# Two channel MLPs of a diffusion backbone on one core: block products by Strassen's seven instead of eight

## The chip, the cores and the metric

The kernel runs on one core of a Trainium2 chip. The metric is the time of one execution on the device in microseconds (us), lower is better. A core has five engines that each run their own queue in order: TensorE (PE, with its weight loads PEld), VectorE (DVE), ScalarE (ACT), GpSimd (POOL) and SyncE (SP), which issues the DMAs. They wait for each other by semaphores.

## The reference, cut to what matters

Two layers work on 1024 tokens of 1024 channels. Each ends in a channel MLP with 4096 hidden channels; layer 0 has retention and attention before it, layer 1 spatial gating.

```python
def sq_relu_mlp(h, w1, w2):
    return jnp.square(jax.nn.relu(h @ w1)) @ w2
...
        x = x + g1 * o_lat
        x = x + g2 * sq_relu_mlp(modulate(rms_norm(x, norm2_g[l]), sh2, sc2), ff_w1[l], ff_w2[l])
```

The six vectors `sh1 .. g2` of a layer come from a product of the conditioning vector with `mod_w`. Everything is float32.

## The kernel before

Tokens lie along the free axis (two halves `hf` of H = 512), channels on the 128 partitions in KT = 8 chunks. A float32 product is made of three matmuls of rounded parts: a value is split into `hi` (an ACT cast) and `lo` (a DVE subtraction), and `mm3` (L53 to L55) multiplies hi*hi, hi*lo and lo*hi into PSUM. PSUM has two buffers of two banks, tag `mm`, and four of one bank, tag `aux`.

The stages follow each other: start, retention projections (`r_group`), attention projections (`a_group`), attention, `out_proj` 0 (tile `po`), MLP 0 (`up`, `dn`, and `dl` for the last group), the gating's products `pv` and `pu`, `out_proj` 1, MLP 1. In an MLP, `up_both` makes one hidden chunk c of 128 channels for both halves: 2 x 24 matmuls into one buffer, then Relu on ACT (L689), a square on DVE (L690) and a split into `s`. `down` takes two chunks at a time into each of the eight output chunks m, 12 matmuls into a buffer of two banks, and DVE adds the buffer, times g2, to the residual `xt[m]` in SBUF (L725). Up of the next chunks and down of the former ones alternate; the last four chunks go half by half (`dl`, L747), with `done` storing each chunk.

`norm_fin` makes the normalised halves as a generator (`later`, `tick`) that is written between the products: sum of squares on ACT and POOL (L166, L167), `nsum` on PE, a power on POOL (L177), a broadcast `nbc` on PE, then two DVE operations and one of ACT per chunk. The first four up tiles of an MLP need the first half only. The modulation vectors other than the first two are 10 parts of 9 steps (`mod_steps`: a 512 KB load and a DVE accumulation of 128x1024 at L117, then transposes), taken one at a time in the projections (`mod_run(1)`) and two at a time in MLP 0 (`mod_run(2)`).

The order on each engine is not the order of the code: the framework's scheduler places instructions, and tiles of a tag are taken in turn from its buffers.

## Time and profile before

| | us |
|---|---|
| three runs | 2440.36, 2443.74, 2444.03 |
| median | 2443.74 |
| span of the profiled execution, first to last instruction | 2437.2 |
| its PE busy | 2387.2 |
| its DVE / ACT / POOL busy | 1280.7 / 683.0 / 178.5 |

The profiled execution is a run of its own. The span is what its page is made from; its time on the device beside the span is not given, and the median of the three runs is 6.5 us over the span. Busy time of PE counts pipelined matmuls whose rows overlap.

### The profile page before, as it was taken

How to read it: one execution, taken by the hardware profiler on the slowest of the kernel's cores; microseconds unless marked ns; L12 is line 12 of the kernel's file. 1: busy time of each engine (PE TensorE's matmuls, PEld its weight loads, DVE VectorE, ACT ScalarE, POOL GpSimd, SP SyncE). 2: the span in 40 equal slices, each digit the busy share in tenths (PEclk: the TensorE clock that was granted, in tenths of full speed). 3: DMA queues.
4: the chain of work that ended last, by engine and by line, in shares of the span. 5: the costliest groups of instructions: out<-in, count | busy, mean ns of one | idle time of the engine just before them, and what ended most of it. 6: DMA issues, size and time to landing. Idle time of an engine off the chain costs nothing.

```text
span 2437.2 us, 27145 instructions
## 1 busy us (share of the span) xinstructions
PE 2387.2 (98%) x11180; PEld 1941.2 (80%) x11180; DVE 1280.7 (53%) x1776; ACT 683.0 (28%) x1131; POOL 178.5 (7%) x143
## 2 busy tenths in 40 slices
...
GB/s 292 121 37 102 106 83 139 120 44 35 147 95 53 72 92 121 51 105 121 26 138 44 65 100 57 48 122 93 59 39 52 52 35 61 44 47 49 44 26 70
DMA packets 67597, 195.38 MB, mean 80 GB/s; under 512 B 7440, under 2 KB 15120, under 8 KB 67472
## 3 DMA queue, kind: packets, MB, share of 16 engines
...
q8 instruction: 88, 1.44, 0.2%
...
## 4 chain that ended last, share of the span: by engine, by line
PE 88%; DVE 5%; DMA 3%; ACT 2%; POOL 1%; issue 1%; SPq 0%; DVEq 0%; POOLq 0%; ACTq 0%
PE up L53 9%; PE up L55 9%; PE up L54 9%; PE dn L55 8%; PE dn L53 8%; PE dn L54 8%; PE po L53 2%; PE po L54 2%; PE po L55 2%; PE pl L55 2%; PE pl L53 2%; PE pl L54 2%; DMA mw<-in_mod_w 2%; PE pv L55 1%; PE dl L53 1%; PE pv L54 1%
## 5 line engine op out<-in xcount | busy, mean ns | idle before, releaser
L58 ACT CAST wh_w<-st_w 128x1024 fp32r<-128x1024 f32 x128 | 132.7, 1050 | 848.9 <-PE dn L54 396.6
L53 PE MATMUL dn<-s,wh_w 128*128 128x512 f32 x896 | 353.8, 395 | 1.6 <-DVE xa L725 1.6
L55 PE MATMUL dn<-s,wl_w 128*128 128x512 f32 x896 | 353.6, 395 | 0.2 <-DVE wl_w L59 0.2
L54 PE MATMUL dn<-s,wh_w 128*128 128x512 f32 x896 | 353.4, 394 | 0.0
L59 DVE TENSOR_TENSOR wl_w<-st_w,wh_w 128x1024 fp32r<-128x1024 f32 x128 | 159.5, 1261 | 316.7 <-ACT wh_w L58 316.1
L725 DVE SCALAR_TENSOR_TENSOR xb<-dn,mcol,xb 128x1024 f32<-128x1024 f32 x112 | 143.6, 1282 | 127.2 <-PE dn L55 127.1
L53 PE MATMUL up<-hm,wh_w 128*128 128x512 f32 x512 | 202.7, 396 | 0.0
L53 PE MATMUL up<-hn,wh_w 128*128 128x512 f32 x512 | 202.5, 395 | 0.0
L55 PE MATMUL up<-hn,wl_w 128*128 128x512 f32 x512 | 202.4, 395 | 0.0
L54 PE MATMUL up<-hn,wh_w 128*128 128x512 f32 x512 | 202.3, 395 | 0.0
L55 PE MATMUL up<-hm,wl_w 128*128 128x512 f32 x512 | 202.3, 395 | 0.0
L54 PE MATMUL up<-hm,wh_w 128*128 128x512 f32 x512 | 202.2, 395 | 0.0
L53 PEld LDWEIGHTS dn<-s,wh_w 128*128 128x128 f32 x896 | 168.7, 188 | 41.4 <-DVE xa L725 2.1
L55 PEld LDWEIGHTS dn<-s,wl_w 128*128 128x128 f32 x896 | 168.7, 188 | 40.2 <-DVE wl_w L59 0.8
L54 PEld LDWEIGHTS dn<-s,wh_w 128*128 128x128 f32 x896 | 168.8, 188 | 39.3
L725 DVE SCALAR_TENSOR_TENSOR xa<-dn,mcol,xa 128x1024 f32<-128x1024 f32 x112 | 143.5, 1282 | 92.5 <-PE dn L55 92.3
L53 PE MATMUL pl<-wh_g,h 128*128 128x512 f32 x384 | 154.0, 401 | 0.0
L55 PE MATMUL pl<-wh_g,h 128*128 128x512 f32 x384 | 151.9, 396 | 0.0
L54 PE MATMUL pl<-wl_g,h 128*128 128x512 f32 x384 | 151.3, 394 | 0.0
L167 POOL TENSOR_TENSOR ss<-ss,sq 128x512 f32<-128x512 f32 x42 | 62.4, 1487 | 1097.1 <-ACT sq L166 1097.1
L689 ACT ACTIVATE r<-up 128x512 f32<-128x512 f32 x128 | 69.9, 591 | 178.4 <-PE up L55 178.3
L690 DVE TENSOR_TENSOR r<-r 128x512 f32<-128x512 f32 x128 | 83.0, 684 | 68.8 <-ACT r L689 68.8
...
## 6 DMA issues: line engine op xcount, KB each, us to landing
st_w<-in_w SPq DMA_DIRECT2D x128, 512.0 KB, 3.6
mw<-in_mod_w SPq DMA_DIRECT2D x96, 512.0 KB, 4.0
st_wo<-in_wo SPq DMA_DIRECT2D x32, 512.0 KB, 3.5
st_g<-in_wg SPq DMA_DIRECT2D x24, 512.0 KB, 4.7
x<-in_xT SPq DMA_DIRECT2D x8, 512.0 KB, 9.6
xa<-in_xT SPq DMA_DIRECT2D x8, 512.0 KB, 7.4
st_wv<-in_wv SPq DMA_DIRECT2D x8, 512.0 KB, 4.2
xp_d<-xa SPq DMA_DIRECT2D x16, 256.0 KB, 2.0
```

The source lines that it names most:

```text
L53: nc.tensor.matmul(ps, lhsT=a_hi, rhs=b_hi, start=first, stop=False)
L54: nc.tensor.matmul(ps, lhsT=a_hi, rhs=b_lo, start=False, stop=False)
L55: nc.tensor.matmul(ps, lhsT=a_lo, rhs=b_hi, start=False, stop=last)
L58: nc.scalar.copy(hi, src)
L59: eng.tensor_tensor(lo, src, hi.bitcast(F32), ALU.subtract)
L167: eng.tensor_tensor(ss, ss, sq, ALU.add)
L689: nc.scalar.activation(r, ps[:, f * H:(f + 1) * H], AF.Relu)
L690: nc.vector.tensor_tensor(r, r, r, ALU.mult)
L725: nc.vector.scalar_tensor_tensor(xt[m], ps.rearrange("p a b -> p (a b)"), mods[(l, 5)][:, m:m + 1], xt[m], ALU.mult, ALU.add)
```

## The change

Both operands of an MLP product are cut into 2x2 blocks and multiplied by Strassen's method in Winograd's form: seven block products for eight, with sums of blocks formed before and after. For the up product, w1 is cut by input chunks (even and odd k) and by pairs of hidden chunks, p = 0 to 15; the tokens are cut into halves. The weight sums `S1 .. S4` are formed on DVE for each p (`w_forms`), the token sums `T1 .. T4` once per MLP (`norm_forms`, which replaces `norm_fin`; `T3` and `T4` on POOL). `block` is one block product: 12 matmuls of 512 columns for four tiles of 128 channels.

Up and down are two phases now. `up_first` makes two of the seven products of p = 0 to 3 from the first half of the tokens and keeps them in DRAM. `mlp_up` makes for each p seven block products in one `mm` buffer (banks a and b) and one `aux` buffer e, adds them up on DVE, takes Relu and Square on ACT, forms the down product's `B` and `T` and stores all seven in DRAM (`s_d`). `mlp_down` loads them again into the 28 buffers of `fpool`, splits them, and works in jobs (q, p0, p1): output chunks q and q + 4, hidden pairs p0 to p1 - 1, at most four. The residual goes to DRAM in `out_proj` (`x1_d`) and comes back as `xd` at the start of the down phase. The norm at the end of layer 0 comes after the whole MLP. The modulation steps all run in the projections. The diff, cut, without its empty lines and the removed functions:

```diff
                 if gi:
-                    mod_run(1)
+                    mod_run(2 + t)
...
+    mod_run(1000)
...
+    FORMS = ("B11", "T2", "B21", "T3", "T1", "T4", "B22")
+    fpool, close_f = open_pool("fpool", side="right", reuse_waits="tile")
+    def f_tile(name, dtype=F32R):
+        return fpool.tile([P, 2, H], dtype, tag="f", bufs=28, name=name)
+    def block(ps, W, F, first):
+        n = len(F)
+        for t in range(n):
+            c = slice(t * P, (t + 1) * P)
+            mm3(ps, W[:, 0, c], W[:, 1, c], F[t][:, 0, :], F[t][:, 1, :], first and t == 0, t == n - 1, not first)
...
+    def w_forms(src, name, skip=False, eng=nc.vector):
+        R1 = w_raw(src(0), f"ra_{name}")
+        R2 = w_raw(src(1), f"rb_{name}")
+        w = R1.shape[-1]
+        f = {}
+        if not skip:
+            f["A11"] = w_form(R1[:, 0], f"w0_{name}")
+        s1 = tmp(f"s1_{name}")[:, :w]
+        eng.tensor_tensor(s1, R2[:, 0], R2[:, 1], ALU.add)
+        s2 = tmp(f"s2_{name}")[:, :w]
+        eng.tensor_tensor(s2, s1, R1[:, 0], ALU.subtract)
+        f["S2"] = w_form(s2, f"w1_{name}")
+        if not skip:
+            f["A12"] = w_form(R1[:, 1], f"w2_{name}")
+        eng.tensor_tensor(R2[:, 0], R1[:, 0], R2[:, 0], ALU.subtract)
+        f["S3"] = w_form(R2[:, 0], f"w3_{name}")
+        f["S1"] = w_form(s1, f"w4_{name}")
+        f["A22"] = w_form(R2[:, 1], f"w5_{name}")
+        eng.tensor_tensor(R1[:, 1], R1[:, 1], s2, ALU.subtract)
+        f["S4"] = w_form(R1[:, 1], f"w6_{name}")
+        return f
...
+                nc.sync.dma_start(x1_d[m, :, sl], xt[m][:, sl])
+                norm_acc(nt, ss[hf], xt[m][:, sl], m == 0)
...
+            later(norm_forms(l, hf, ss[hf], xt, F))
...
+    def norm_forms(l, hf, ss, xt, F):
+        sl = slice(hf * H, (hf + 1) * H)
+        rs = norm_rstd(nt, ss, H)
+        yield 1
+        pb = norm_bc(rs, H)
+        gs, sh = mods[(l, 4)], mods[(l, 3)]
+        for t in range(4):
+            for j in range(2):
+                k = 2 * t + j
+                x = xt[k][:, sl]
+                nc.vector.scalar_tensor_tensor(x, x, gs[:, k:k + 1], pb, ALU.mult, ALU.mult)
+                nc.scalar.activation(x, x, AF.Identity, bias=sh[:, k:k + 1])
+            def form(n, src, eng=nc.vector):
+                o = f_tile(f"{n}_{l}_{t}")
+                F.setdefault(n, []).append(o)
+                split(src, o[:, 0, :], o[:, 1, :], eng)
+            if hf == 0:
+                form("B11", xt[2 * t][:, sl])
+                form("B21", xt[2 * t + 1][:, sl])
+            else:
+                b11, b21 = xt[2 * t][:, 0:H], xt[2 * t + 1][:, 0:H]
+                b12, b22 = xt[2 * t][:, H:], xt[2 * t + 1][:, H:]
+                t1, t2 = tmp(f"t1_{l}{t}"), tmp(f"t2_{l}{t}")
+                nc.vector.tensor_tensor(t1, b12, b11, ALU.subtract)
+                nc.vector.tensor_tensor(t2, b22, t1, ALU.subtract)
+                form("T2", t2)
+                nc.gpsimd.tensor_tensor(b12, b22, b12, ALU.subtract)
+                form("T3", b12, nc.gpsimd)
+                form("T1", t1)
+                nc.gpsimd.tensor_tensor(b21, b21, t2, ALU.subtract)
+                form("T4", b21, nc.gpsimd)
+                form("B22", b22)
+            yield 1
+    def mlp_up(l, F, s_d, utemp, pro):
+        def src(p):
+            return lambda i: I["w1"][l, p, i]
+        for p in range(16):
+            f = w_forms(src(p), f"u{l}_{p}", skip=p in pro)
+            ps = mm_tile([P, 2, H], f"up{l}_{p}")
+            a, b = ps[:, 0, :], ps[:, 1, :]
+            e = aux_tile([P, H], f"ue{l}_{p}")
+            def act(t):
+                nc.scalar.activation(t, t, AF.Relu)
+                nc.scalar.activation(t, t, AF.Square)
+            def put(n, t):
+                nc.sync.dma_start(s_d[p][FORMS.index(n)], t)
+            e1, s11 = utemp(f"e1_{l}_{p}"), utemp(f"s11_{l}_{p}")
+            if p in pro:
+                nc.sync.dma_start(e1, pro[p])
+                nc.sync.dma_start(s11, s_d[p][0])
+            else:
+                block(a, f["A11"], F["B11"], True)
+                nc.scalar.copy(e1, a)
+            block(b, f["S2"], F["T2"], True)
+            u2 = utemp(f"u2_{l}_{p}")
+            nc.vector.tensor_tensor(u2, b, e1, ALU.add)
+            if p not in pro:
+                block(a, f["A12"], F["B21"], False)
+                nc.scalar.activation(s11, a, AF.Relu)
+                nc.scalar.activation(s11, s11, AF.Square)
+                put("B11", s11)
+            block(b, f["S3"], F["T3"], False)
+            u3 = utemp(f"u3_{l}_{p}")
+            nc.vector.tensor_tensor(u3, b, e1, ALU.add)
+            block(e, f["S1"], F["T1"], True)
+            nc.vector.tensor_tensor(u3, e, u3, ALU.add)
+            act(u3)
+            put("B22", u3)
+            block(b, f["A22"], F["T4"], False)
+            nc.vector.tensor_tensor(e1, b, e1, ALU.add)
+            act(e1)
+            block(e, f["S4"], F["B22"], False)
+            nc.vector.tensor_tensor(u2, e, u2, ALU.add)
+            act(u2)
+            t1, t2 = utemp(f"q1_{l}_{p}"), utemp(f"q2_{l}_{p}")
+            nc.vector.tensor_tensor(t1, u2, s11, ALU.subtract)
+            put("T1", t1)
+            nc.vector.tensor_tensor(t2, u3, t1, ALU.subtract)
+            put("T2", t2)
+            nc.vector.tensor_tensor(u2, u3, u2, ALU.subtract)
+            put("T3", u2)
+            t4 = utemp(f"q4_{l}_{p}")
+            nc.vector.tensor_tensor(t4, e1, t2, ALU.subtract)
+            put("B21", e1)
+            put("T4", t4)
+    def up_first(l, F, s_d, e_d):
+        for p0 in (0, 2):
+            ps = mm_tile([P, 2, H], f"uf{l}_{p0}")
+            W = []
+            for d in range(2):
+                R = w_raw(I["w1"][l, p0 + d, 0], f"rf{l}_{p0 + d}")
+                W.append([w_form(R[:, j], f"wf{l}_{p0 + d}_{j}") for j in range(2)])
+            for d in range(2):
+                block(ps[:, d, :], W[d][0], F["B11"], True)
+                e1 = tmp(f"ef{l}_{p0 + d}")
+                nc.scalar.copy(e1, ps[:, d, :])
+                nc.sync.dma_start(e_d[p0 + d], e1)
+            for d in range(2):
+                block(ps[:, d, :], W[d][1], F["B21"], False)
...
+    def mlp_down(l, xt, s_d, done):
         S = {}
+        def load_s(p):
+            S[p] = {}
+            for i, n in enumerate(FORMS):
+                o = f_tile(f"s{n}_{l}_{p}")
+                lo = o[:, 1, :]
+                nc.sync.dma_start(lo.bitcast(F32), s_d[p][i])
+                split(lo.bitcast(F32), o[:, 0, :], lo)
+                S[p][n] = o
+        def job(q, p0, p1):
+            for p in range(p0, p1):
+                if p not in S:
+                    load_s(p)
+            F = {n: [S[p][n] for p in range(p0, p1)] for n in FORMS}
...
+            f = w_forms(lambda i: I["w2"][l, q, i, :, :, p0:p1], name)
...
+            x11, x12 = xt[q][:, :H], xt[q][:, H:]
+            x21, x22 = xt[q + 4][:, :H], xt[q + 4][:, H:]
+            ps = mm_tile([P, 2, H], f"dn{name}")
+            a, b = ps[:, 0, :], ps[:, 1, :]
+            e = aux_tile([P, H], f"de{name}")
...
+            block(a, f["A11"], F["B11"], True)
+            e1, e2 = tmp(f"e1{name}"), tmp(f"e2{name}")
+            nc.scalar.activation(e1, a, AF.Copy, scale=g1)
+            nc.scalar.activation(e2, a, AF.Copy, scale=g2)
+            add(x21, e2)
+            block(b, f["S2"], F["T2"], True)
+            stt(e1, b, g1, e1)
+            add(x12, e1)
+            block(a, f["A12"], F["B21"], False)
+            stt(x11, a, g1, x11)
+            block(b, f["S3"], F["T3"], False)
+            stt(e2, b, g2, e2)
+            add(x22, e2)
+            block(e, f["S1"], F["T1"], True)
+            stt(x22, e, g2, x22)
+            block(b, f["A22"], F["T4"], False)
+            stt(x21, b, g2, x21)
+            block(e, f["S4"], F["B22"], False)
+            stt(x12, e, g1, x12)
...
+        job(1, 0, 1)
+        job(2, 0, 2)
+        job(3, 0, 3)
+        for i in range(16):
+            job(i % 4, i, min(i + 4, 16))
+    def layer_mlp(l, F, close_xt, s_d, e_d, x1_d, done):
+        up_first(l, F, s_d, e_d)
+        drain()
+        close_xt()
+        up, close_up = open_pool("up", reuse_waits="tile")
+        mlp_up(l, F, s_d, lambda n: up.tile([P, H], F32, tag="u", bufs=16, name=n), {p: e_d[p] for p in range(4)})
+        close_up()
+        xd, close_xd = open_pool("xd", reuse_waits="tile")
+        xt = [xd.tile([P, T], F32, name=f"xd{l}_{m}") for m in range(KT)]
+        for m in range(KT):
+            nc.sync.dma_start(xt[m], x1_d[m])
+        mlp_down(l, xt, s_d, lambda q: done(q, xt))
+        return close_xd, xt
...
+    close_xd, xt = layer_mlp(0, F, close_xa, s_d, e_d, x1_d, done0)
+    hm = [[None] * KT for _ in range(2)]
+    for hf in range(2):
+        rs = norm_rstd(nt, ss1[hf], H)
+        pb = norm_bc(rs, H)
```

**Place 1, the start of MLP 0.** POOL's queue before, where the norm of the second half ends; `ss001` is its sum of squares, `rs` the power, `ss010` the sum at the end of MLP 0.

```order
L167 TENSOR_TENSOR ss001_5523<-ss001_5523,sq_6096 128x512 [waits Activation_49,Pool_49]
L167 TENSOR_TENSOR ss001_5523<-ss001_5523,sq_6131 128x512 [waits Activation_49,Pool_49]
L177 TENSOR_TENSOR rs_6200<-ms_6198,mhalf_76 128x4 [waits DVE_49]
L167 TENSOR_TENSOR ss010_6138<-ss010_6138,sq_10363 128x512 [waits PE_49,Activation_49]
L167 TENSOR_TENSOR ss010_6138<-ss010_6138,sq_10381 128x512 [waits Activation_49,Pool_49]
```

POOL's queue now; `xa` are the residual's chunks, which hold the normalised tokens at this point (second half: b12, b22).

```order
L168 TENSOR_TENSOR ss001_5752<-ss001_5752,sq_6384 128x512 [waits Activation_49,Pool_49]
L178 TENSOR_TENSOR rs_6552<-ms_6550,mhalf_76 128x4 [waits DVE_49]
L746 TENSOR_TENSOR xa0_5722<-xa1_5723,xa0_5722 128x512 [waits DMAHW1_49,DMAHW0_49,DMAHW6_49,DVE_49,Activation_49]
L749 TENSOR_TENSOR xa1_5723<-xa1_5723,t2_00_6564 128x512 [waits DMAHW3_49,DVE_49]
L746 TENSOR_TENSOR xa2_5724<-xa3_5725,xa2_5724 128x512 [waits DMAHW2_49,DMAHW4_49,DVE_49,Activation_49]
L59 TENSOR_TENSOR T3_0_0_6571<-xa0_5722,T3_0_0_6571 128x512 [waits DMAHW7_49,Activation_49]
...
L746 TENSOR_TENSOR xa6_5728<-xa7_5729,xa6_5728 128x512 [waits DMAHW2_49,DMAHW1_49,DVE_49]
L59 TENSOR_TENSOR T4_0_2_6628<-xa5_5727,T4_0_2_6628 128x512 [waits PE_49,Activation_49]
L749 TENSOR_TENSOR xa7_5729<-xa7_5729,t2_03_6639 128x512 [waits DVE_49]
L59 TENSOR_TENSOR T3_0_3_6646<-xa6_5728,T3_0_3_6646 128x512 [waits PE_49,Activation_49]
L59 TENSOR_TENSOR T4_0_3_6653<-xa7_5729,T4_0_3_6653 128x512 [waits PE_49,Activation_49]
```

Sixteen operations of 128x512 now stand behind the power (rows of t = 1 and 2 in between are left out). ACT's queue at the same place, before: `hm0_1` are the chunks of the second half, `r` and `s0` belong to up tiles.

```order
L195 ACTIVATE hm0_1_4_5518<-hp_6297,mcol03_2069 128x512 [waits DVE_49]
L195 ACTIVATE hm0_1_5_5519<-hp_6301,mcol03_2069 128x512 [waits DVE_49]
L689 ACTIVATE r_6344<-up0_3_0_6319 128x512 [waits DVE_49,PE_49,Pool_49]
L195 ACTIVATE hm0_1_6_5520<-hp_6305,mcol03_2069 128x512 [waits DVE_49]
L195 ACTIVATE hm0_1_7_5521<-hp_6309,mcol03_2069 128x512 [waits DVE_49]
L58 CAST s0_3_0_6347<-r_6344 128x512 [waits DVE_49]
```

And now; `w1_u0_0` is W S2 of p = 0, which `up0_0`, the first tile of `mlp_up`, needs.

```order
L58 CAST T2_0_3_6642<-t2_03_6639 128x512 [waits DVE_49]
L58 CAST T3_0_3_6646<-xa6_5728 128x512 [waits Pool_49]
L58 CAST T1_0_3_6649<-t1_03_6638 128x512
L58 CAST T4_0_3_6653<-xa7_5729 128x512 [waits Pool_49]
L58 CAST B22_0_3_6656<-xa7_5729 128x512
L58 CAST w1_u0_0_6671<-s2_u0_0_6669 128x512 [waits DVE_49]
```

The cast of the first weight form stands behind casts that wait for POOL.

**Place 2, the middle of the up phase, PE.** Before: `up0_8` is one hidden chunk, its halves go into its two banks, `up0_9` takes the other buffer.

```order
L55 MATMUL dn0_4_7_7136<-s0_5_1_6735,wl_w2_0_5_7035 128x512
L53 MATMUL up0_8_7156<-hm0_0_0_5506,wh_w1_0_8_7152 128x512 [waits DVE_49]
...
L55 MATMUL up0_8_7156<-hm0_0_7_5513,wl_w1_0_8_7153 128x512
L53 MATMUL up0_8_7156<-hm0_1_0_5514,wh_w1_0_8_7152 128x512
...
L55 MATMUL up0_8_7156<-hm0_1_7_5521,wl_w1_0_8_7153 128x512
L53 MATMUL up0_9_7229<-hm0_0_0_5506,wh_w1_0_9_7225 128x512 [waits DVE_49,Activation_49]
```

Now: `up0_6` is the buffer of p = 6 with banks a and b, `ue0_6` and `ue0_8` are e of p = 6 and 8, `w1` to `w6` the weight forms S2, A12, S3, S1, A22, S4.

```order
L55 MATMUL up0_6_7460<-T2_0_3_6642,w1_u0_6_7440 128x512
L53 MATMUL up0_6_7460<-B21_0_0_6138,w2_u0_6_7443 128x512 [waits DVE_49]
...
L55 MATMUL up0_6_7460<-B21_0_3_6276,w2_u0_6_7443 128x512
L53 MATMUL up0_6_7460<-T3_0_0_6571,w3_u0_6_7447 128x512 [waits Activation_49]
...
L55 MATMUL up0_6_7460<-T3_0_3_6646,w3_u0_6_7447 128x512
L53 MATMUL ue0_8_7759<-T1_0_0_6574,w4_u0_8_7748 128x512 [waits Activation_49]
L53 MATMUL up0_6_7460<-T4_0_0_6578,w5_u0_6_7453 128x512 [waits DVE_49]
...
L55 MATMUL up0_6_7460<-T4_0_3_6653,w5_u0_6_7453 128x512
L53 MATMUL ue0_6_7461<-B22_0_0_6581,w6_u0_6_7457 128x512 [waits DVE_49]
```

Four blocks on one buffer stand behind each other, each with a wait for DVE or ACT at its first matmul; before, a tile's two halves ran through and the wait of the next tile was for the other buffer.

**Place 3, the change from up to down, PE.** Before, the first down tiles: `dn0_0_0` and `dn0_0_1` are output chunks 0 and 1 of the first two hidden chunks.

```order
L55 MATMUL up0_3_1_6443<-hm0_1_7_5521,wl_w1_0_3_6316 128x512
L53 MATMUL dn0_0_0_6486<-s0_0_0_6190,wh_w2_0_0_6476 128x512 [waits DMAHW1_49,DMAHW7_49,DMAHW0_49,Activation_49]
...
L55 MATMUL dn0_0_0_6486<-s0_1_1_6409,wl_w2_0_1_6483 128x512
L53 MATMUL dn0_0_1_6500<-s0_0_0_6190,wh_w2_0_0_6476 128x512 [waits Activation_49]
...
L55 MATMUL dn0_0_1_6500<-s0_1_1_6409,wl_w2_0_1_6483 128x512
L53 MATMUL dn0_0_2_6514<-s0_0_0_6190,wh_w2_0_0_6476 128x512 [waits DVE_49]
```

Now: `ue0_15` ends the up phase, `dnd0_2_0` is the buffer of job (2, 0, 2), `dnd0_1_0` that of job (1, 0, 1), `ded0_3_0` the e of job (3, 0, 3).

```order
L55 MATMUL ue0_15_8802<-B22_0_3_6656,w6_u0_15_8798 128x512
L53 MATMUL dnd0_2_0_9093<-sB11_0_0_8939,w0_d0_2_0_9066 128x512 [waits DVE_49]
...
L55 MATMUL dnd0_2_0_9093<-sB11_0_1_9034,w0_d0_2_0_9066 128x512
L53 MATMUL dnd0_2_0_9093<-sT2_0_0_8943,w1_d0_2_0_9073 128x512 [waits Activation_49]
...
L55 MATMUL dnd0_2_0_9093<-sT2_0_1_9038,w1_d0_2_0_9073 128x512
L53 MATMUL dnd0_2_0_9093<-sB21_0_0_8947,w2_d0_2_0_9076 128x512 [waits DVE_49]
...
L55 MATMUL dnd0_2_0_9093<-sB21_0_1_9042,w2_d0_2_0_9076 128x512
L53 MATMUL ded0_3_0_9210<-sT1_0_0_8955,w4_d0_3_0_9199 128x512 [waits Activation_49]
...
L55 MATMUL ded0_3_0_9210<-sT1_0_2_9166,w4_d0_3_0_9199 128x512
L53 MATMUL dnd0_1_0_8998<-sT3_0_0_8951,w3_d0_1_0_8985 128x512 [waits DVE_49]
```

Blocks of six matmuls on one buffer follow each other, each with a wait at its head, where tiles of twelve with two buffers in turn stood before.

## Rows read from the trace of the kernel before

**Rows 1.** The page: busy us, share of the span, instructions, per engine.
```profile
PE 2387.2 (98%) x11180; PEld 1941.2 (80%) x11180; DVE 1280.7 (53%) x1776; ACT 683.0 (28%) x1131; POOL 178.5 (7%) x143
```
**Rows 2.** Windows of MLP 0, MLP 1 and its end: columns in the first row.
```profile
core 0: us, PE busy (x) PEld busy (x) DVE busy (x) ACT busy (x) POOL busy (x), PEclk, DMA share, GB/s
702.00:1382.00 680.00, 678.19 (x2945) 547.80 (x2945) 358.63 (x378) 138.59 (x193) 2.80 (x2) 1.00 0.25 81
...
1716.00:2388.00 672.00, 672.00 (x2897) 543.41 (x2896) 299.26 (x313) 135.70 (x192) 3.02 (x2) 1.00 0.14 44
2388.00:2437.00 49.00, 45.43 (x195) 36.10 (x193) 14.61 (x20) 2.31 (x4) 0.00 (x0) 1.00 0.23 86
```
**Rows 3.** Timeline of PE in MLP 1: start, duration; first and last of 25.
```profile
1799.75 0.39 PE L53 MATMUL up<-hn,wh_w 128*128 128x512 f32 x1
...
1805.35 0.39 PE L53 MATMUL up<-hn,wh_w 128*128 128x512 f32 x1
```
**Rows 4.** The page's costliest groups: busy us, mean ns, idle before and its releaser.
```profile
L53 PE MATMUL dn<-s,wh_w 128*128 128x512 f32 x896 | 353.8, 395 | 1.6 <-DVE xa L725 1.6
...
L53 PE MATMUL up<-hm,wh_w 128*128 128x512 f32 x512 | 202.7, 396 | 0.0
```
**Rows 5.** Timeline near the kernel's end: the last matmul of a tile and its evacuation.
```profile
2430.30 0.40 PE L55 MATMUL dl<-s,wl_w 128*128 128x512 f32 x1
...
2430.53 0.39 PE L53 MATMUL dl<-s,wh_w 128*128 128x512 f32 x1
...
2430.74 0.75 DVE L747 SCALAR_TENSOR_TENSOR xb<-dl,mcol,xb 128x512 f32<-128x512 f32 x1 [2.04 <-PE dl L55]
```
**Rows 6.** Timeline in the gating: two DVE operations and the matmul that waited.
```profile
1528.66 2.36 DVE L824 TENSOR_TENSOR zg<-zg,vr 128x1024 f32<-128x1024 f32 x2 [1.81 <-POOL vr L812]
1529.93 0.49 PE L832 MATMUL psv<-wsT,zg 128*128 128x128 f32 x2 [1.37 <-DVE zg L824]
```
**Rows 7.** DVE's groups by shape in MLP 1.
```profile
L59 DVE TENSOR_TENSOR s<-r,s 128x512 fp32r<-128x512 f32 x62 | 40.3, 686 | 4.0 <-ACT s L58 2.7
...
L194 DVE SCALAR_TENSOR_TENSOR hp<-xb,mcol,nbc 128x512 f32<-128x512 f32 x8 | 5.8, 740 | 0.0
L674 DVE SCALAR_TENSOR_TENSOR xb<-po,mcol,xb 128x512 f32<-128x512 f32 x1 | 0.8, 751 | 3.5 <-PE po L55 3.5
```
**Rows 8.** ACT's groups by shape in `out_proj` 0 and MLP 0.
```profile
L58 ACT CAST s<-r 128x512 fp32r<-128x512 f32 x64 | 39.2, 621 | 30.1 <-DVE r L690 30.1
L689 ACT ACTIVATE r<-up 128x512 f32<-128x512 f32 x64 | 35.0, 592 | 151.0 <-PE up L55 151.0
```
**Rows 9.** POOL's groups by shape, whole span.
```profile
L167 POOL TENSOR_TENSOR ss<-ss,sq 128x512 f32<-128x512 f32 x42 | 62.4, 1487 | 1097.1 <-ACT sq L166 1097.1
...
L475 POOL TENSOR_TENSOR zrl<-ropea,ropeb 128x512 f32<-128x512 f32 x16 | 21.5, 1343 | 131.2 <-DVE ropeb L380 123.3 <-DVE po L307 4.8 <-PE kv L493 3.1
...
L177 POOL TENSOR_TENSOR rs<-ms,mhalf 128x4 f32<-128x4 f32 x6 | 9.7, 1615 | 16.8 <-DVE ms L175 16.8
...
L59 POOL TENSOR_TENSOR h<-x,h 128x512 fp32r<-128x512 f32 x2 | 2.9, 1439 | 3.3 <-ACT h L58 3.3
```
**Rows 10.** The page's DMA issues: count, KB each, median us to landing.
```profile
xa<-in_xT SPq DMA_DIRECT2D x8, 512.0 KB, 7.4
...
xp_d<-xa SPq DMA_DIRECT2D x16, 256.0 KB, 2.0
```
**Rows 11.** Windows around a standstill of PE in the attention projections, columns as in rows 2.
```profile
446.00:450.00 4.00, 0.00 (x0) 0.00 (x0) 2.79 (x7) 1.72 (x4) 1.36 (x1) 0.75 0.93 358
...
453.00:456.00 3.00, 1.99 (x10) 2.00 (x11) 3.00 (x7) 1.82 (x5) 0.00 (x0) 0.50 0.00 0
...
459.00:462.00 3.00, 2.73 (x13) 1.94 (x12) 1.81 (x5) 2.49 (x7) 0.00 (x0) 1.00 0.53 172
```
**Rows 12.** Timeline of PE behind that standstill.
```profile
455.99 0.63 PE L54 MATMUL s<-wl_ak,wh_aq 128*128 128x512 f32 x1
456.42 0.63 PE L55 MATMUL s<-wh_ak,wl_aq 128*128 128x512 f32 x1
```
**Rows 13.** Groups of the whole span: the accumulation of a modulation step.
```profile
L117 DVE SCALAR_TENSOR_TENSOR macc<-mw,scc,macc 128x1024 f32<-128x1024 f32 x70 | 91.6, 1308 | 31.9 <-DMA mw<-in_mod_w 31.6
```
**Rows 14.** Window of the first attention group, columns as in rows 2.
```profile
340.00:398.00 58.00, 56.11 (x326) 48.94 (x325) 48.47 (x90) 15.83 (x24) 7.96 (x7) 1.00 0.48 147
```

235 lines of the change are left out of this document (96 added, 139 removed).

## The prediction

> **What bounds the kernel now.** I read the page's busy shares first: TensorE 2387.2 us of a span of 2437.2, the next engine 53% [rows 1]. The stage windows show where a matmul saved can still be given back: in the two MLPs PE is busy in 678.19 of 680.00 us and in 672.00 of 672.00, at granted clock 1.00, and their ends add 48 and 49 us [rows 2]. The timeline gives the price of a matmul: 24 steps of 128x512 from 1799.75 to 1805.35, 0.2333 us each (a row's 0.39 overlaps the next) [rows 3]. A layer's 3072 matmuls make 716.7 us by it; 672.0 + 45.4 were measured for layer 1. The groups show no waits in front of them: 1.6 us before 896 matmuls [rows 4]. So PE is the bound, with every evacuation under other matmuls: each accumulation fills its own buffer and PE goes on in the next. Every wait that the change brings to PE in these stages is paid in full, and every matmul taken out is saved in full.
>
> The profile's span is 2437.2, the runs' median 2443.7; I sum differences and add them to the median.
>
> **What it removes.** Seven block products for eight: 2688 matmuls for 3072, 384 x 0.2333 = 89.6 us per layer, **-179.2** [rows 3]. The Trainium skill (TensorE: Matmul & The Clock Gate, section Wait — 56ns, not 53.3ns?) gives 215.7 ns from start to start for 512 columns at 2.4 GHz. By that the saving would be an estimated 165.7 and the sum 13.5 us higher; the rows of this kernel differ, and they decide.
>
> **What it adds, by following the new order with durations of rows.** A 128x512 operation takes 0.69 us on DVE (0.75 with a PSUM operand and three inputs) [rows 7], 0.6 on ACT [rows 8], 1.44 to 1.49 as a two-input operation on POOL [rows 9]. When PE has to wait for an evacuation: the last matmul starts at 2430.30, DVE at 2430.74, that is 0.21 behind the slot in which the next matmul would go [rows 5]; back from DVE to PE it is 0.09 us (the first of two operations that take 2.36 from 1528.66 ends at 1529.84, PE starts at 1529.93) [rows 6]. An exposed evacuation costs PE 0.21 + 0.69 + 0.09 = 1.0 us on DVE, 0.9 on ACT.
>
> *Start of each MLP.* Before, the norm of the second half lay under four up tiles that need only the first (22 us). Now 96 matmuls of `up_first` (22.4 us) are the cover, and the work behind them is longer. Count from the end of the output projection: `nsum` stands behind 60 matmuls (14.0 us), the pow takes 1.6, the last `nbc` stands behind 12 more matmuls, 19.7. Eight DVE operations of 0.74 bring 25.8, t1 26.5, and POOL starts its chain: 14 operations up to the last b21 - t2, at 1.44, 46.7. The ACT queue stands in order: the cast of T4_3 waits for that, behind it B22_3 and then W S2 of p = 0, 48.6; DVE subtracts three times, 50. PE had 22.4 + 0.8 us of work and waits for W S2: **27 us per layer**. If POOL goes at its best row of this kind (1.34 us, a mean I saw for another line) it is 25, with DVE beside it at 1.49, 28; 22 to 34 holds the rest. After such a gap the clock is low: behind the standstill of 446 to 450 the granted clock is 0.50 (1.2 GHz) up to 456 and 1.00 (2.4 GHz) from 459 [rows 11], with 512 columns every 0.43 us on the way [rows 12]. Six us at half rate cost 3. Both layers: 54 + 6 = **+60**.
>
> *p = 0 to 3.* DVE has 20 operations (13.7 us) for 60 matmuls (14.0), and q2, u2, q4 of one p stand ahead of the next one's u2; PE meets waits of 3.2 us (before S1*T1 of p = 4) and 3.7 (before S3*T3 of p = 3) and some of 0.5 to 1.0: 8 per layer (3 to 14), **+16**.
>
> *p = 4 to 15.* Here lies the largest term. a and b are two banks of one tile `up`, and each block on that tile waits for what was evacuated from it last, whichever bank. The order puts S2*T2, A12*B21, S3*T3 and A22*T4 of one p behind each other, with one matmul between the last two. So the second waits for u2, the third for the Relu, the fourth for u3: 1.0 + 0.9 + 1.0, less 0.2 for the one matmul, is 2.7 us, and I add 0.3 for a DVE that comes late: 3.0 per p instead of none. 12 x 3.0 = 36 per layer, **+72**. Bounds: 1.0 if two of the three are covered, 4.4 if DVE, 13.7 us of work in a period of 19.6, is late each time.
>
> *From up to down.* The 28 slots hold F forms until the last blocks of p = 15; then 28 loads of a form, w2 and eight reloads of xd come together. The jobs (1,0), (2,0), (3,0) have blocks of 3, 6 and 9 matmuls (0.7 to 2.1 us) that follow each other on one tile and cover nothing, DVE stands behind q stores and S splits, and the first stt on xd waits for the reload, which is issued behind the q stores: a store takes 2.0, a 512 KB load under load 7.4 [rows 10]. Counted from the last matmul of p = 15: A11*B11 of job (2,0) ends at 1.4; S2*T2 waits for ACT, which has the Relu and Square of u2 first (to 4.2, 2.8 lost); A12*B21 for an stt behind q1, s2, q2, u2, q4 on DVE (to 7.6, 2.0 lost); S1*T1 of job (3,0) for its W form (1.3); S3*T3 of job (1,0) for the first stt on xd, behind fourteen splits and form steps on DVE (to 16.9, 3.8); its A22*T4 for e2, which waits for POOL's add on xd5, the sixth reload in the queue (to 22.2, 3.2); then 3 us in smaller ones. That is 16 us beside 32 of matmuls, and 3 more where job (1,0) lies beside p = 14: 19 per layer (10 to 30), **+38**.
>
> *Down.* 13 jobs are full: 84 matmuls 19.6 us, DVE 18 x 0.69 + 6 x 0.75 = 16.9, ACT 16 x 0.62 = 9.9, POOL 3 x 1.49 = 4.5. Here the order puts 5 or 6 matmuls of another tile (1.2 to 1.4 us) between blocks of one tile, more than the 0.9 to 1.0 of an evacuation, and a form's slot is free one period before its next use. I take 0.4 per job, 5 per layer, **+10** (0 to 39 per layer, below); narrow jobs at the end 4 per layer, **+8**.
>
> *Layer 0's end.* The norm of half 0 no longer lies beside half 1's products. Squares, POOL adds, pow and broadcast are some 6 us, then eight pairs of DVE operations at 0.74 feed pv's first tile (12 us against 5.6 of matmuls): **+12**. The last store is 512 KB instead of 256: **+2**.
>
> *Modulation steps* move from MLP 0 to the projections: 12 more per group x 1.31 us [rows 13]. The retention groups' DVE has room; in the first attention group DVE is busy 48.47 of 58 us [rows 14] and 12 x 1.31 = 15.7 come on top, 6.2 more than fit. MLP 0 loses them, and was 8.0 us longer than MLP 1 [rows 2]. Together **0** (-8 to +15). The rest of the transfers I cost at nothing: a period of either phase moves nine transfers, 2.9 MB in 19.6 us, 147 GB/s, which is what the first attention group moved with its DMA engines busy 48% [rows 14]; were they late by 1 us a job, that is 26 us.
>
> Sum: -179.2 + 60 + 16 + 72 + 38 + 10 + 8 + 14 = +39. **2443.7 + 39 = 2483 us**, slower.
>
> **Rivals.** *The waits in p = 4 to 15 are mostly covered, and it is faster.* Place: between blocks of one `up` tile. With 0.2 us at each of the three instead of 0.9, and no late DVE, 2.4 x 24 = 58 of the 72 go, and half of the p = 0 to 3 waits: 2443.7 + 39 - 58 - 8 = 2417. It decides where a period of these p falls under 21.0 us (3.0 - 39/24 = 1.4 us of waits). For it: DVE and ACT are 53% and 28% busy, and a queue that I took as late may catch up in the 27-us gap. Against: PE keeps the program's order and the waits stand in its rows. *DVE becomes the bound in the down phase.* At 16.9 of 19.6 us it needs to lose only 16%, to POOL beside it or to a wait for a form; 3 us per job cost 26 x 3 = 78: 2561. Against: in the MLPs before its rows beside ACT and DMA do not stretch. *The clock falls in the up phases.* If the short waits bring the low level over p = 4 to 15 of both layers, 2016 matmuls take 0.43 instead of 0.2333: +397, 2880. Against: the low rows stand behind a standstill of 4 us in which PE did nothing [rows 11], and PE is busy for 88% of such a period.
>
> The Trainium skill (TensorE: Matmul & The Clock Gate, section A second HAM failure mode: psum-queue depth-cycling) says that a kernel whose PE idles briefly between groups while it cycles through PSUM banks went back and forth between the clock's two levels. That is the third rival's rule; by it the up phases would run as slow as worked out there. No row here shows it for waits under 1 us.
>
> *Nothing changes to speak of*, gains and waits meeting within 5 us, has no mechanism of its own.
>
> **How the numbers follow.** My forecast (2445 to 2525) 0.56; covered waits 0.25; DVE bound 0.13; the clock 0.02; a tie 0.04. A measurement of this kernel can tell about 0.2%, 5 us. Faster 0.25, same 0.04, slower 0.71. The range leaves out the clock and the outer parts of the two others: 2400 to 2570.
>
> **What would show it.** PE's rows by tile: waits of `up` before DVE u2, u3 and ACT s11 of 0.8 to 1.0 us each, 24 per kind; a gap of 24 to 30 us before the first `up` block in each layer, with POOL busy throughout; a down job every 19.6 to 20.5 us; a total of PE busy near 2210. I would be wrong if periods of p = 4 to 15 stand under 21 us, if the gap at the start is under 15, or if down jobs take over 22.

## The result and the profile after

The changed kernel takes 2637.53 us (median of four runs, 2631.57 to 2643.38) against 2443.89 of the kernel before on the same chip: ratio 1.0795, 95% interval 1.0776 to 1.0815. The forecast of 2483 us (2400 to 2570) had the direction, slower, but not the size: the change cost 194 us instead of 39, and the time lies outside the range. The profiled execution has a span of 2633.7 us.

The page of the changed kernel, its engines' busy time and TensorE's granted clock in 40 slices, against [rows 1]:

```profile
PE 2320.2 (88%) x10412; PEld 1806.1 (69%) x10412; DVE 1715.3 (65%) x2670; ACT 1044.5 (40%) x1881; POOL 413.4 (16%) x289
...
PEclk9999999899989999989999969999799999899999
```

PE is busy for 67 us less and the span is 196.5 us longer: PE stands idle for 313 us, where it was idle for 50. The first matmul of each stage says where:

| stretch, us | before | after | difference |
|---|---|---|---|
| up to `out_proj` 0 (start, projections, attention) | 610.5 | 639.2 | +28.7 |
| `out_proj` 0 | 91.7 | 95.4 | +3.7 |
| MLP 0 with the norm up to `pv` | 727.5 | 815.7 | +88.2 |
| gating products | 195.1 | 207.7 | +12.6 |
| `out_proj` 1 | 91.3 | 91.2 | -0.1 |
| MLP 1 up to the end | 721.1 | 784.4 | +63.3 |

The windows of the changed kernel's MLPs, against [rows 2]. Per layer: the start with p = 0 to 3; p = 4 to 14; the last p and four jobs; eleven full jobs; the rest.

```profile
734.60:865.40 130.80, 88.63 (x353) 67.69 (x351) 88.22 (x114) 53.46 (x91) 28.64 (x18) 0.86 0.32 111
865.40:1113.20 247.80, 224.31 (x924) 171.04 (x924) 143.26 (x229) 109.05 (x184) 0.00 (x0) 1.00 0.39 133
1113.20:1215.70 102.50, 81.52 (x295) 59.07 (x296) 72.47 (x114) 43.05 (x81) 16.57 (x12) 0.90 0.58 190
1215.70:1456.90 241.20, 225.42 (x926) 169.60 (x925) 193.78 (x264) 101.45 (x178) 50.52 (x34) 1.00 0.42 129
1456.90:1550.40 93.50, 65.73 (x236) 46.76 (x234) 48.91 (x70) 26.47 (x51) 37.28 (x27) 0.82 0.30 104
...
1849.30:1980.70 131.40, 89.61 (x353) 68.75 (x351) 88.20 (x115) 53.44 (x91) 29.17 (x18) 0.83 0.33 110
1980.70:2230.60 249.90, 225.54 (x925) 171.74 (x925) 143.12 (x229) 108.98 (x184) 0.00 (x0) 0.99 0.39 132
2230.60:2332.20 101.60, 80.67 (x294) 58.34 (x295) 72.20 (x114) 43.17 (x81) 16.58 (x12) 0.92 0.57 192
2332.20:2572.10 239.90, 225.12 (x925) 169.64 (x924) 192.98 (x264) 101.45 (x177) 50.36 (x34) 1.00 0.42 130
2572.10:2633.70 61.60, 52.84 (x211) 38.76 (x209) 35.01 (x60) 11.09 (x27) 15.53 (x12) 0.94 0.21 81
```

A period of p = 4 to 14 is 22.5 us in layer 0 and 22.7 in layer 1 for 84 matmuls (19.6 us at 0.2333), a full down job 21.9 and 21.8. PE loses time in every stretch, and no other engine is near its whole time. PE's waits in the changed kernel, largest first (in total, times, longest), against [rows 4], where 1.6 us stood before 896 matmuls:

```profile
PE up L53 <- ACT w_u L58: 57.7, 2, 28.9
PE up L53 <- DVE u L780: 30.4, 25, 6.1
PE dnd L53 <- DVE xd L858: 22.0, 28, 3.4
PE dnd L53 <- DVE e1d L858: 18.8, 23, 2.2
PE up L53 <- ACT s L783: 15.7, 23, 1.0
PE ue L53 <- ACT w_u L58: 15.6, 22, 0.7
...
PE pv L53 <- ACT zg L966: 9.5, 1, 9.5
```

The first row is the two gaps at the start of the MLPs. Rows two, five and six are the waits of the up phase: three kinds, 22 to 25 times each. One period of them, PE's timeline (what ended the wait in brackets):

```profile
925.62 0.50 PE L53 MATMUL up<-B,w_u 128*128 128x512 f32 x1 [0.78 <-DVE u L780]
...
929.37 0.50 PE L53 MATMUL up<-T,w_u 128*128 128x512 f32 x1 [0.69 <-ACT s L783]
...
933.15 0.50 PE L53 MATMUL ue<-T,w_u 128*128 128x512 f32 x1 [0.71 <-ACT w_u L58]
```

From 925.62 to 933.15 two blocks of 12 matmuls take 7.53 us instead of 5.6. The third row names ACT: `ue` is the first matmul of a later p, the cast of its weight form runs from 932.48, and it waited for a weight buffer that the block before had just read. DVE's u3, which was expected there, runs from 932.48 too and ends with the cast, so the rows don't tell whether u3 alone would have made the same gap.

The down phase has a cost that no MLP of the kernel before shows. POOL's adds of one job, and DVE beside them:

```profile
1328.47 1.42 POOL L861 TENSOR_TENSOR xd<-xd,e2d 128x512 f32<-128x512 f32 x1 [6.78 <-ACT e2d L866]
1332.99 1.67 POOL L861 TENSOR_TENSOR xd<-xd,e1d 128x512 f32<-128x512 f32 x1 [3.10 <-DVE e1d L858]
```

```profile
1328.05 0.69 DVE L684 TENSOR_TENSOR s_d<-s_d,ra_d 128x512 f32<-128x512 f32 x1
1328.93 1.51 DVE L59 TENSOR_TENSOR sB<-sB 128x512 fp32r<-128x512 f32 x1 [0.19 <-ACT sB L58]
1330.37 0.68 DVE L688 TENSOR_TENSOR rb_d<-ra_d,rb_d 128x512 f32<-128x512 f32 x1
...
1333.44 1.77 DVE L59 TENSOR_TENSOR sB<-sB 128x512 fp32r<-128x512 f32 x1
1335.13 0.68 DVE L59 TENSOR_TENSOR w_d<-rb_d,w_d 128x512 fp32r<-128x512 f32 x1
```

A split that takes 0.69 us elsewhere takes 1.51 and 1.77 when it starts while POOL adds: the first ends 0.55 us behind POOL (POOL's end at 1329.89, DVE's at 1330.44), a little under its own length, and so does the second. Over the trace, the 24 splits `sB` that start beside a POOL operation take 1.72 us in the mean, the 72 others 0.69; the evacuations of L858, which read PSUM, take 0.75 either way. The Trainium skill (SBUF — State Buffer, section Who interferes with whom) says that a DVE instruction with two SBUF inputs and a GpSimd instruction that reads SBUF exclude each other, and that one with at most one SBUF input, outside DVE's two-port modes, is not touched. These rows agree.

How this reaches PE: in the two windows of eleven full jobs PE waits 50 times for over 0.1 us, each time for a DVE evacuation, 30.5 us in all. Each time DVE came to that evacuation straight from other work, and in 35 of the 50 this unbroken stretch of work holds at least one operation that POOL had held up. No idle time of DVE in the window of layer 0 ends on POOL, so the result of POOL's adds is not what DVE was late for.

### The profile page after: what moved, and what is told of

It reads as the page before. It is cut to its first block, busy times and chain, and to the rows that moved or that the text cites. A ratio compares the mean times of both kernels' runs of the same rounds, so it can differ in the third digit from the quotient of the medians.

```text
span 2633.7 us, 29088 instructions
## 1 busy us (share of the span) xinstructions
PE 2320.2 (88%) x10412; PEld 1806.1 (69%) x10412; DVE 1715.3 (65%) x2670; ACT 1044.5 (40%) x1881; POOL 413.4 (16%) x289
## 5 line engine op out<-in xcount | busy, mean ns | idle before, releaser
L53 PE MATMUL up<-T,w_u 128*128 128x512 f32 x384 | 161.1, 420 | 92.8 <-ACT w_u L58 57.7
L53 PE MATMUL dnd<-sT,w_d 128*128 128x512 f32 x384 | 164.2, 428 | 45.5 <-DVE xd L858 22.0
L861 POOL TENSOR_TENSOR xd<-xd,e2d 128x512 f32<-128x512 f32 x76 | 102.1, 1345 | 381.4 <-DVE e2d L858 203.5
L53 PEld LDWEIGHTS up<-T,w_u 128*128 128x128 f32 x384 | 75.2, 196 | 125.2 <-ACT w_u L58 58.6
L55 PE MATMUL up<-T,w_u 128*128 128x512 f32 x384 | 156.7, 408 | 0.0
L54 PE MATMUL up<-T,w_u 128*128 128x512 f32 x384 | 156.6, 408 | 0.0
L54 PE MATMUL dnd<-sT,w_d 128*128 128x512 f32 x384 | 155.9, 406 | 0.0
L55 PE MATMUL dnd<-sT,w_d 128*128 128x512 f32 x384 | 155.8, 407 | 0.0
L53 PEld LDWEIGHTS dnd<-sT,w_d 128*128 128x128 f32 x384 | 74.1, 193 | 95.6 <-DVE xd L858 37.5
L58 ACT CAST sT<-sT 128x512 fp32r<-128x512 f32 x128 | 78.8, 619 | 132.9 <-DMA sT<-s_d 128.8
L59 DVE TENSOR_TENSOR sT<-sT 128x512 fp32r<-128x512 f32 x128 | 94.9, 751 | 45.7 <-ACT sT L58 45.4
L53 PE MATMUL dnd<-sB,w_d 128*128 128x512 f32 x256 | 105.0, 410 | 19.2 <-DVE e1d L858 18.8
L118 DVE SCALAR_TENSOR_TENSOR macc<-mw,scc,macc 128x1024 f32<-128x1024 f32 x70 | 92.6, 1323 | 23.5 <-DMA mw<-in_mod_w 23.1
L59 DVE TENSOR_TENSOR sB<-sB 128x512 fp32r<-128x512 f32 x96 | 90.8, 946 | 20.7 <-ACT sB L58 20.2
L58 ACT CAST w_d<-ra_d 128x512 fp32r<-128x512 f32 (+3 forms) x114 | 61.5, 551 | 102.9 <-DVE ra_d L692 83.2
L54 PE MATMUL dnd<-sB,w_d 128*128 128x512 f32 x256 | 101.6, 397 | 0.0
L55 PE MATMUL dnd<-sB,w_d 128*128 128x512 f32 x256 | 100.2, 397 | 0.0
```

Source lines behind the costliest of these rows:

```text
L53: nc.tensor.matmul(ps, lhsT=a_hi, rhs=b_hi, start=first, stop=False, skip_group_check=more)
L54: nc.tensor.matmul(ps, lhsT=a_hi, rhs=b_lo, start=False, stop=False, skip_group_check=more)
L55: nc.tensor.matmul(ps, lhsT=a_lo, rhs=b_hi, start=False, stop=last, skip_group_check=more)
L58: nc.scalar.copy(hi, src)
L59: eng.tensor_tensor(lo, src, hi.bitcast(F32), ALU.subtract)
L118: nc.vector.scalar_tensor_tensor(acc, st, scc[:, k, 0:1], acc, ALU.mult, ALU.add)
```

## The experiments

Each changes the changed kernel, except where another is named. "Lost" is the time of a stretch less its matmuls at 0.2333 us; of the 19 down jobs of a layer, three are narrow at the start, 13 full, and three (jobs 16 to 18) narrow at the end.

### One part each: banks, adds, modulation steps

**e1_up_banks.**

```diff
-            ps = mm_tile([P, 2, H], f"up{l}_{p}")
-            a, b = ps[:, 0, :], ps[:, 1, :]
+            a = aux_tile([P, H], f"ua{l}_{p}") if p not in pro else None
+            b = mm_tile([P, H], f"up{l}_{p}")
```

> Changed kernel with one edit: in the up phase the accumulators a and b are two tiles (a in a one-bank buffer of tag aux, b in a buffer of tag mm) instead of the two banks of one tile. Theory A: the 3.0 us that each p of 4 to 15 loses in the changed kernel (22.6 us a period for 19.6 us of matmuls) are waits between blocks that share the tile. Then the periods fall to 19.6 to 20.0 and the time falls by 24 x 2.8 = 67 us, some 5 more at p = 0 to 3: about 2565. Rival B: DVE or the loads of w1 are late as well and take the place of the waits: periods stay above 21.5, the time falls by under 30 us.

2535.31 us (ratio to the kernel before 1.0386, 95% interval 1.0363 to 1.0409; so in brackets below), 102 us less than the changed kernel. PE in a window from p = 5 to 14:

```profile
884.90:1081.70 196.80, 196.80 (x842) 157.41 (x841) 128.57 (x204) 98.20 (x166) 0.00 (x0) 1.00 0.43 145
```

Ten periods take 19.68 us each; PE has no idle time, with the same work on DVE and ACT. Theory A holds, rival B falls. Summed over both layers, p = 4 to 15 lost 84.4 us and lose 13.8 (6.0 of it at each p = 4); p = 0 to 3 lost 35.4 and lose 10.9, the first three jobs 43.5 and now 34.2. Theory A expected 72 us in all; what came on top is mostly in p = 0 to 3 and the first jobs. The waits were set for the tile, whichever of its banks a block wrote: in the rows above `up<-B`, which writes bank a, waits for u2, which reads bank b. With two tiles PE did without them. The scheduler also put the blocks in another order (blocks of `ua` and `ue` now stand between those on `up`, and the wait for the weight cast is gone as well), so the run shows what the shared tile cost with its order, not each of the three waits by itself.

**e2_down_banks**, the same in `mlp_down`.

```diff
-            ps = mm_tile([P, 2, H], f"dn{name}")
-            a, b = ps[:, 0, :], ps[:, 1, :]
+            a = aux_tile([P, H], f"da{name}")
+            b = mm_tile([P, H], f"dn{name}")
```

> Changed kernel with one edit: in the down phase a and b are two tiles, as above. Full down jobs take 21.9 us in the changed kernel for 19.6 us of matmuls. Theory C: these 2.3 us are waits between blocks of one tile, as in the up phase: jobs fall to 19.6 to 20.2, the time by 40 to 50 us, about 2590. Rival D: DVE is late because its operations with two SBUF inputs wait for POOL's adds (0.69 us becomes 1.1 to 1.8), and blocks on b alone still wait for it: jobs stay at 21 or more, the time falls by under 20 us.

2585.87 us (1.0584, 1.0567 to 1.0602), 52 less. But the 26 full jobs lost 1.3 us each instead of 2.2, 22 us of the 52; 13 came from the last two p, which the first jobs now overlap, and 13 from the narrow jobs at the end. So C had the total and not the reason: more than half of a full job's loss stayed.

**e3_adds_on_dve.**

```diff
             def add(x, u):
-                nc.gpsimd.tensor_tensor(x, x, u, ALU.add)
+                nc.vector.tensor_tensor(x, x, u, ALU.add)
```

> Changed kernel with one edit: the three adds onto the residual in each down job are on DVE instead of POOL. Rival D (DVE held by POOL): the 3 x 0.69 us that DVE gets are about what it loses now to POOL (2.1 us a job), the splits are 0.69 again, and the end comes forward where a split was held: jobs fall to about 20.5 to 21, the time by 20 to 35 us. Theory C (blocks of one tile wait for their evacuation wherever DVE stands): jobs stay within 0.5 us of 21.9, the time within 13 us, or it gets longer because the adds stand ahead of evacuations in DVE's queue.

2587.88 us (1.0596, 1.0571 to 1.0622), 50 less; full jobs lost 0.7, which is 38 of the 50, and the narrow jobs at both ends 7 less each. The two kinds of split in full jobs, first the changed kernel, then this one:

```profile
L59 DVE TENSOR_TENSOR sB<-sB 128x512 fp32r<-128x512 f32 x33 | 35.1, 1062 | 7.3 <-ACT sB L58 7.1
L59 DVE TENSOR_TENSOR sT<-sT 128x512 fp32r<-128x512 f32 x44 | 33.1, 757 | 19.0 <-ACT sT L58 19.0
```

```profile
L59 DVE TENSOR_TENSOR sT<-sT 128x512 fp32r<-128x512 f32 x44 | 30.3, 689 | 12.8 <-ACT sT L58 12.3
L59 DVE TENSOR_TENSOR sB<-sB 128x512 fp32r<-128x512 f32 x34 | 23.4, 689 | 6.8 <-ACT sB L58 6.6
```

Work moved onto the busier engine, and the kernel got faster, by more than the 20 to 35 us expected: theory D, with a larger share of a job's loss (1.5 of 2.2) than the shared tile (0.8).

**e4_mods_alone** is the kernel before with one part of the change.

```diff
-                    mod_run(1)
+                    mod_run(2 + t)
...
+    mod_run(1000)
     close_tabs()
```

> The kernel before with one part of the change: all modulation steps in the projections. Theory E: the 28.8 us by which the output projection of layer 0 starts later in the changed kernel come from this part alone: 512 KB loads of the steps stand in SP's queue and in the three staging tiles ahead of the weights of the next group. Then this kernel's output projection starts 25 to 30 us later too, MLP 0 gives back about 8 us, and it is 17 to 22 us slower than before: about 2463. Rival F: the other edits ahead of that place (pools, buffers) make it: it stays within 8 us of before.

2462.73 us against 2441.3 (1.0080, 1.0064 to 1.0096): +21.4. Its `out_proj` 0 starts at 637.9 (before 610.5), and MLP 0 takes 7.8 us less. Theory E holds: this part alone costs 27.4 us up to `out_proj` 0 and gives 7.8 back. How, at one place: the turn from the first to the second retention group. SP's queue before, then in the changed kernel:

```profile
106.68 13.95 SPq L63 DMA_DIRECT2D st_g<-in_wg  x4
```

```profile
87.86 78.49 SPq L114 DMA_DIRECT2D mw<-in_mod_w  x14
...
172.79 14.25 SPq L63 DMA_DIRECT2D st_g<-in_wg  x4
```

The four weight loads of the second group take the same 14 us to issue in both kernels, but now they stand 66 us later, behind sixteen loads of modulation steps (fourteen in the row shown, two at 167.34) that pass through the same three staging tiles. DVE in the changed kernel:

```profile
193.36 3.43 DVE L59 TENSOR_TENSOR wl_g<-st_g,wh_g 128x1024 fp32r<-128x1024 f32 x2
196.72 1.41 DVE L118 SCALAR_TENSOR_TENSOR macc<-mw,scc,macc 128x1024 f32<-128x1024 f32 x1
```

The last splits of the weights end at 196.8. The group's first matmuls, `pc`, run through only from 195.7, after a few at 182.9 and at 188.2; before, they ran through from 183.6. The other turns were not read in this way, so for them the mechanism is argued.

### The start of an MLP

**e5_first8** and **e6_forms_early** build on e1_up_banks.

```diff
-        for p0 in (0, 2):
+        for p0 in (0, 2, 4, 6):
```

> Kernel of e1_up_banks with one more edit: the blocks that need only the first half of the tokens are made ahead for p = 0 to 7 instead of 0 to 3 (192 matmuls of cover, 44.8 us, instead of 22.4). Theory G: the 29.0 us before the first other up block, in each layer, are a chain of fixed length (norm, forms on DVE and POOL, ACT's queue) that ends later than its cover; then the gap falls to 6 to 10 us, and with DVE at 13.7 us of work per 14.0 us for eight p instead of four 5 us a layer are given back: about 2505. Rival H: what ends last is DVE's whole work from the norm to p = 3 or 7; then the waits come back at p = 1 to 8 and the time stays within 12 us of e1_up_banks.

2600.86 us (1.0652, 1.0626 to 1.0678): 65 us slower than e1_up_banks. Neither theory gave that time. The broadcast of the norm, on PE, in the changed kernel and in this one (first matmuls of the phase at 734.6 and 734.3):

```profile
756.24 0.39 PE L184 MATMUL nbc<-ident,rs 128*128 128x128 f32 x2
```

```profile
775.64 0.39 PE L184 MATMUL nbc<-ident,rs 128*128 128x128 f32 x2
```

In PE's queue the broadcast had gone behind the added matmuls, 41.3 us into the phase instead of 21.6. The chain behind it began 20 us later and the gap stayed (26.8 us). So the cover gained nothing at the gap. The 65 us came behind it: p = 0 to 8 then lost 44 us a layer (12 in e1_up_banks), with PE waiting for DVE's evacuations, up to 5.1 us at a time. These are the waits that rival H named, at a far higher price.

The edit of e6_forms_early, cut:

```diff
-                nc.gpsimd.tensor_tensor(b12, b22, b12, ALU.subtract)
-                form("T3", b12, nc.gpsimd)
+            for t in range(4):
+                b12, b22 = xt[2 * t][:, H:], xt[2 * t + 1][:, H:]
+                nc.vector.tensor_tensor(b12, b22, b12, ALU.subtract)
+                form("T3", t, b12)
+            for t in range(4):
+                form("T1", t, xt[2 * t][:, 0:H])
...
+        f0 = w_forms(lambda i: I["w1"][l, 0, i], f"u{l}_0", skip=True)
         drain()
```

> Kernel of e1_up_banks with one more edit: the token forms are made kind by kind (T2 of all four first), all on DVE, and the weight forms of p = 0 are written ahead of the norm. Theory G: the first block then waits for 8 products with the norm and 12 operations for t1, t2, T2 on DVE, not for POOL's fourteen and the casts behind them; the gap falls from 29.0 to 7 to 12 us, later forms cost 5 to 10 us, together 10 to 20 us a layer: about 2505. Rival H: DVE has 16 operations more (11 us) and is what ends last; the time stays within 12 us of e1_up_banks.

2518.09 us (1.0310, 1.0291 to 1.0330), 17 less than e1_up_banks. The gap fell from 29 us to waits of 6.0 and 7.3; but the start with p = 0 to 4 lost 37 us a layer instead of 46. Theory G had the gap; its later costs were higher than it said, and the gain of 17 us for both layers lies under its 10 to 20 us a layer.

What filled the gap in the changed kernel, POOL's first operations (of 16) in it:

```profile
762.75 1.30 POOL L746 TENSOR_TENSOR xa<-xa,xa 128x512 f32<-128x512 f32 x1 [11.69 <-DVE t L743]
...
766.30 1.71 POOL L746 TENSOR_TENSOR xa<-xa,xa 128x512 f32<-128x512 f32 x1
767.97 1.71 POOL L59 TENSOR_TENSOR T<-xa,T 128x512 fp32r<-128x512 f32 x1
```

The first of them finds DVE between two operations and takes 1.30; the others of the run take 1.64 to 1.72, and DVE's beside them mostly 1.75 instead of 0.69. The two engines alternate here, and each waits for the other.

### The end of layer 0, and everything together

**e7_norm_later.**

```diff
             stt(x21, b, g2, x21)
+            if late:
+                done(late.pop())
...
-                done(q)
+                late.append(q)
```

> Changed kernel with one edit: the squares and sums for the norm at the end of layer 0 (and the stores) of a job are written after the second-last evacuation of the next job instead of at its own end. Theory I: jobs 16 to 18 of layer 0 lose 6.1, 10.1 and about 10 us, those of layer 1 1.5, 0.6 and 4.9, because ACT's squares wait for the residual at the head of its queue, with the next job's weight casts behind them; then the jobs of layer 0 lose 2 to 6 us each and the time falls by 12 to 20 us: about 2620. Rival J: POOL's sums hold DVE's splits wherever the squares stand: the time stays within 6 us of the changed kernel.

2623.20 us (1.0737, 1.0714 to 1.0761), 14 less. Jobs 16 and 17 of layer 0 lose 2.8 and 5.5 us instead of 6.1 and 10.1. Theory I. In the changed kernel, ACT and DVE at job 17 show both causes, the squares ahead of the weight casts and then POOL's sums (three from 1500.46, 4.16 us) beside splits that take 0.41 us alone:

```profile
1499.76 1.67 ACT L167 ACTIVATE sq<-xd 128x512 f32<-128x512 f32 x3 [8.01 <-DVE xd L858]
...
1501.90 0.39 ACT L58 CAST w_d<-s_d 128x256 fp32r<-128x256 f32 x1
```

```profile
1502.32 1.16 DVE L59 TENSOR_TENSOR w_d<-s_d,w_d 128x256 fp32r<-128x256 f32 x1 [1.46 <-ACT w_d L58]
1503.41 1.50 DVE L59 TENSOR_TENSOR w_d<-ra_d,w_d 128x256 fp32r<-128x256 f32 x1
```

**e8_all_but_start** joins e1, e2, e3 and e7, and moves four parts of the modulation between the gating products.

```diff
-                    mod_run(2 + t)
+                    mod_run((1 + t) if (1, 1) not in mods else 0)
...
                 nc.scalar.activation(zg[cg * 4 + j][:, tt, :], ps[:, j, :], AF.Gelu_apprx_tanh)
+            if cg or tt > 1:
+                mod_run(2)
```

> Changed kernel with five edits together: a and b as two tiles in both phases, the three adds on DVE, the norm's squares a job later, and the modulation steps of layer 1 that the gating does not need moved into the gating's products. If the terms add up: 2637 less 102 (e1_up_banks), less 26 x 2.0 = 52 for full jobs, less 15 for the norm, less 10 to 15 for the modulation steps: 2453 to 2460, still slower than before by the 60 us at the start of the two MLPs. If they overlap (the adds on DVE compete with evacuations that now cover each other): 2480 to 2500.

2429.93 us (0.9947, 0.9929 to 0.9966): 0.5% faster than before, and 23 us under the lower expectation. Twelve full jobs:

```profile
1128.60:1365.70 237.10, 236.35 (x1009) 188.87 (x1008) 200.44 (x325) 107.05 (x191) 0.00 (x0) 1.00 0.45 140
```

19.76 us a job, PE idle for 0.75 us in all, DVE busy for 85%. The two reasons for a job's loss were separate, and in these jobs both are gone; over all 26 full jobs 0.6 us each is left, half of it in the first of each layer. `out_proj` 0 starts at 608.9, 30 us earlier, and the gating products take 216.9 instead of 207.7: the modulation steps gave 21 us and not 10 to 15.

**e9_forms_early** is e8 with the edit of e6. **e10_first6** is e9 with more made ahead and the norm's steps written between:

```diff
-        for p0 in (0, 2):
+        for p0 in (0, 2, 4):
...
                 nc.sync.dma_start(s_d[p0 + d][0], s11)
+            tick()
```

> Kernel of e8_all_but_start with the edit of e6_forms_early (token forms kind by kind on DVE, weight forms of p = 0 ahead of the norm). Theory: the start is a stretch of its own and the terms add up: 2430 less the 17 us of e6_forms_early, 2413. Rival: the modulation steps and the banks have already changed what ends last there; the time stays within 5 us of e8_all_but_start.

2420.30 us (0.9908, 0.9893 to 0.9924), 9.6 us under e8: between the sum of the terms (17) and the rival (under 5).

> Kernel of e9_forms_early with two edits: the blocks of the first half are made ahead for p = 0 to 5, and the norm's sum and broadcast are written between them (after the first and the second pair) instead of behind them. Theory K: in e5_first8 the gap stayed because PE runs in order and the broadcast of the norm had moved behind the added matmuls (41.5 us after the start of the phase instead of 21.7), so the chain began 20 us later; with the broadcast at 15 to 17 us and 33.6 us of cover, the gap (6.0 and 7.3 us of waits in e6_forms_early) goes to under 4 us and the time falls by 10 to 25 us: about 2395. Rival H: DVE's whole work from the norm to p = 5 ends last; the waits come back at p = 1 to 6 and the time stays within 8 us of e9_forms_early or is over it.

2452.12 us (1.0034, 1.0021 to 1.0046), 32 us slower than e9. The gap went, as theory K said (no wait there is over 4.8 us), but rival H decides. PE's largest waits:

```profile
PE up L53 <- DVE u L788: 28.0, 8, 4.8
PE up L53 <- ACT w_u L58: 15.9, 4, 4.6
```

Eight waits for DVE; the start with p = 0 to 6 loses 54 us a layer, the same stretch of e9 40. From 757 to 790 us DVE is busy for 29.05 of 33 us. That what ends last is DVE's queue from the norm on, and that every block made ahead brings weight splits into it sooner, fits this and e5, but no run changed that queue alone.

**e11_fill_gap** is e8 with 116 matmuls a layer that nothing reads.

```diff
         drain()
+        dm = aux_tile([P, H], f"dm{l}")
+        for i in range(116):
+            nc.tensor.matmul(dm, lhsT=F["B11"][0][:, 0, 0:P], rhs=F["B21"][0][:, 0, :], start=i == 0, stop=i == 115)
```

> Kernel of e8_all_but_start with 116 matmuls more per layer, 27.1 us, written behind the blocks made ahead, into a PSUM buffer that nothing reads: TensorE is busy in the gap before the first other up block instead of standing still for 29 us. Theory L: the gap's length is the chain's and does not change; what changes is the granted clock, 0.50 in the gap and until 3.8 us behind it, and the matmuls that ran at 0.43 us instead of 0.2333 (1.7 us in layer 0, 2.3 in layer 1) run at the higher level: 3 to 5 us faster, about 2426. Rival: the extra matmuls end later than the chain or hold the norm's broadcast up on PE, and the time rises by 4 us or more.

2457.20 us (1.0063, 1.0049 to 1.0077), 27 slower than e8; in the traces the two MLPs take 24 us more. The gap's end did not move (58.6 us into the phase, 58.2 in e8), and the granted clock was 1.00 under the fill. But a wait of 4.5 us was left behind it, with the clock at 0.62 from 772.5 to 777, and the second up block now waited 7.9 us. DVE in this kernel:

```profile
775.96 0.68 DVE L59 TENSOR_TENSOR w_u<-ra_u,w_u 128x512 fp32r<-128x512 f32 x1
779.91 0.69 DVE L683 TENSOR_TENSOR s_u<-rb_u 128x512 f32<-128x512 f32 x1 [3.27 <-DMA rb_u<-in_w]
```

The scheduler had put the weight sums of p = 1 ahead of the first evacuation u2 in DVE's queue, and they waited for their load. So the price of the clock is not measured by this run; it stays with the count below.

**e12_gating_norm** is e9 with the second half's norm as a generator beside the first gating tiles. For that the gating's own buffers are opened four tiles later, and the modulation steps begin three tiles later, three at a time instead of two.

```diff
-    for hf in range(2):
-        rs = norm_rstd(nt, ss1[hf], H)
+    def norm_hm(hf):
+        rs = norm_rstd(nt, ss1[hf], H)
+        yield 1
...
+    later(norm_hm(0))
+    drain()
+    later(norm_hm(1))
+    tick()
...
+            tick()
```

> Kernel of e9_forms_early with one more edit: at the end of layer 0 the second half of the tokens is normalised step by step between the first gating tiles, as in the kernel before, instead of ahead of them. Theory M: the third gating tile waited 9.5 us because its buffer's Gelu stood in ACT's queue behind the casts of the second half, which wait for DVE; that wait goes, and with it 7 to 10 us: about 2411. Rival: the second half is then what the fifth tile waits for; under 3 us.

2407.71 us (0.9856, 0.9841 to 0.9872), 12.6 under e9. Gating products 206.2 us instead of 216.2; the wait of 9.5 us for `zg` is gone. This is the best version that was run: 1.4% faster than the kernel before. Its MLP 0 takes 709.7 us up to `pv` and MLP 1 693.9, against 727.5 and 721.1: of the 179 us of matmuls saved, 45 arrive in the MLPs.

## Why the prediction was wrong, step by step

The terms of the sum for both layers, and what they measured in the changed kernel:

| term | predicted | measured |
|---|---|---|
| matmuls removed | -179.2 | -179.2 |
| start of each MLP up to the first other block | +60 | +70.0 |
| p = 0 to 3 | +16 | +35.4 |
| p = 4 to 15, and the first three jobs | +110 | +127.9 |
| full jobs | +10 | +56.1 |
| narrow jobs, layer 0's end with the gating products, last store | +22 | +61.5 |
| modulation steps | 0 | +20.9 |
| `out_proj` 0 | 0 | +3.7 |

The last jobs and ends measured 56.3 lost and 12.6 in the gating products, less 7.4 that the kernel before lost at its own ends; the modulation steps are 28.7 less the 7.8 of e4. The column sums to 196.3, the spans differ by 196.5.

*The largest term was right.* Three waits of 0.7 to 0.8 us and 3.0 lost per p stood in the trace (periods of 22.6 us in the mean; above the 21.0 that would have decided for the first rival), and e1 took them away. At one of the three the row names a weight buffer and not u3.

*"Down ... I take 0.4 per job"* is the step that failed most: 2.2 us were lost per full job, 56 us in all and 46 more than predicted. It took DVE's 16.9 us of work at 0.69 an operation, and gave the second rival 0.13 because "in the MLPs before its rows beside ACT and DMA do not stretch". True, and no evidence: POOL was busy 2.80 and 3.02 us in those stretches [rows 2]. The change itself puts POOL beside DVE. Rows of the kernel before did show it elsewhere. In `out_proj` 0, POOL and DVE:

```profile
676.11 1.30 POOL L167 TENSOR_TENSOR ss<-ss,sq 128x512 f32<-128x512 f32 x1 [4.88 <-ACT sq L166]
```

```profile
676.47 2.01 DVE L59 TENSOR_TENSOR wl_w<-st_w,wh_w 128x1024 fp32r<-128x1024 f32 x1
```

This split takes 2.06 us in the six rows that start beside a POOL operation and 1.22 in the 122 others. That, and the rule of the Trainium skill quoted above, spoke against the change, and neither is in the prediction. What the runs showed in place of 0.4: DVE held up by POOL's adds costs 1.5 us a job (e3) and the shared tile 0.8 (e2). The rival had the first mechanism; its form (DVE the bound, 3 us a job) was not what came: DVE is busy 80% of a job, and late for single evacuations.

*"Layer 0's end ... +12"* with the narrow jobs: 39.5 us too little. It counted the chain behind the last job and not where its squares stand in ACT's queue (e7: 14 us), nor that the second half's norm stands there ahead of the Gelu of `pv` (e12: 10 us). The two causes of the full jobs are in these jobs too: e2 took 13 us off them and e3 7.

*"Modulation steps ... together 0"* compared DVE's busy time with the stage. The loss, 20.9 us net (e4: 21.4), came with the loads: at the turn that was read the weights stood 66 us later in SP's queue, while DVE was busy for only 37 of the 56 us around it.

*The start*: the gap was 29 us where 27 was predicted, and part of that is luck. POOL's operations took 1.71 us beside DVE where 1.44 was counted, and the chain ended 58.2 us into the phase instead of 50; but the cover also ended later, at 29.3 us instead of 23.2, and the two errors nearly cancel. p = 0 to 3 had waits of 10 us a layer where 8 was predicted, and the clock cost more than the 3 us a layer: up to the end of p = 3, rows at the low level make 4.1 us in layer 0 and 5.4 in layer 1. The gap and two stretches behind it in the changed kernel (granted clock is the third number from the end):

```profile
763.60:792.80 29.20, 0.34 (x2) 0.00 (x0) 29.00 (x22) 12.91 (x24) 25.49 (x16) 0.59 0.05 18
792.80:796.60 3.80, 3.80 (x9) 2.62 (x10) 3.80 (x7) 2.18 (x4) 0.00 (x0) 0.55 0.22 69
796.60:800.00 3.40, 3.40 (x16) 2.51 (x15) 1.19 (x3) 0.00 (x0) 0.00 (x0) 1.00 0.80 247
```

Nine matmuls in 3.8 us, then sixteen in 3.4. It fell again behind the wait of 6.1 us at p = 3, and the turn to down has 0.90 and 0.92 in its windows. A row of 512 columns takes 0.43 us from start to start at the low level. Counting rows 0.38 to 0.52 us apart without a wait between them, and leaving out the vector products `modrow` at the kernel's start: 167 in the changed kernel, 32.5 us over 0.2333; 19 and 3.6 us before. That is 29 us, spread over the terms, for the 6 predicted.

*The third rival* fell: with three waits in each period the clock was 1.00 over p = 4 to 14 of layer 0 and 0.99 in layer 1. The rule of the Trainium skill (TensorE: Matmul & The Clock Gate, section A second HAM failure mode: psum-queue depth-cycling) did not show for waits of 0.8 us. Longer ones had their price: the 0.99 comes from one stretch at 0.50 behind a wait of 1.91 us.

```profile
2066.00:2069.40 3.40, 2.87 (x7) 1.67 (x6) 0.00 (x0) 0.49 (x2) 0.00 (x0) 0.50 0.00 0
```

None of the three conditions named for being wrong came about (periods under 21, a start gap under 15, jobs over 22 in the mean). Of the four signs that it named, the waits and the gap came; a job every 19.6 to 20.5 us and PE busy for near 2210 us did not (21.9, and 2320.2, of which the rows at the low level explain 29). The error lay in stretches for which no such condition was named.
